# A decoder step on one core: the products with a pair of value pages are issued half a key step later

## The chip, the cores and the metric

The kernel runs on one core of a Trainium2 chip. The metric is device time in microseconds (us) of one execution, the median of several. The engines are TensorE (PE in the profile, with its weight loads as PEld), VectorE (DVE), ScalarE (ACT), GpSimd (POOL) and SyncE (SP). Each takes its instructions in a fixed order, and they wait for one another through semaphores. Sixteen DMA engines carry the transfers that the queues start.

## The reference, cut to what matters

One layer of a decoder is applied to two groups of rows with the same weights: a prompt of 1024 rows, and 8 samples of one row each. The samples attend to a paged cache of 8192 past tokens, 64 pages of 128 tokens for each sample, with 8 heads of 64 numbers:

```python
k_all = concatenate([k_pool[page_table], k]); v_all = concatenate([v_pool[page_table], v])
c = cumsum(concatenate([logf_pool[page_table], logf]))
s = einsum('bqhd,bkhd->bhqk', q, k_all) * HD**-0.5 + (c_q - c_k)
out = einsum('bhqk,bkhd->bqhd', softmax(s), v_all)
```

So for each sample all keys come first (scores), then a softmax over 8192 tokens, then all values (weighted sum). Keys and values of 8 samples are 256 blocks of 1 MB. The prompt goes through an input projection, causal attention, spatial gating, an output projection, cross-attention into 256 memory rows, and a gated MLP with a short convolution; the samples go through the same layers after their attention.

## The kernel before, in words

All is float32. The prompt's products are made of three matmuls each, of a rounded operand and its remainder (`gemm3`, lines 272 to 274); the weights come in blocks of 512 KB on SP's queue and are split by ACT (L235) and DVE (L236).

Two programs are woven into one. The prompt's, called the main program here, is a Python generator that goes through seven stages: p1 (input projection), att0 and attx, att1 (attention of the two halves of the rows), mid0 and ffn0 (projection, cross-attention and MLP of the first half), mid1 and ffn1 (the second). Each of its `yield`s hands over a label of how much TensorE time the step just issued is worth: 5.2 for a product with 24 matmuls of 512 columns, 3.9 for one of the down projection, 1 to 1.8 in attention. The samples' program is a second generator, called the decode, followed by the rest (the samples' other layers).

The loop at L1913 adds up the labels of the main program. When a stage's price (`PACE`, L76) has been reached, it takes one turn of the decode and subtracts the price times what that turn yields. Two limits matter here. A main step gives at most `int(t / price) + 1` turns, and while `held[0]` is set (around the norms) it gives none, so that labels pile up. The prices per whole step are 7.0 in p1, 12 in att0, 26 in attx, 11 in att1, 8.0 in mid0, 8.5 in ffn0, 6.8 in mid1, 2.5 in ffn1, and 2.9 for the rest.

The decode runs over `g` from 0 to 147. For each of the 8 samples there are 16 key steps. A key step (`kstep`, L1417) fetches 1 MB of keys by an indirect DMA on POOL's queue (L1420) and makes 4 x 8 scores for each partition on DVE: a multiply (L1436, or L1427 in attention) and a reduction (L1440, or L1428). In the attention stages it is cut into four parts with a yield of 0.2 before each; elsewhere it is one turn. Eighteen steps later come the values: after every second key step two blocks are fetched (`vstep`, L1479; its DMA is L1482), and the function that is to make their products is put on the list `pend`. In the next key step, behind that step's scores, both functions are called, the later block first. Each issues four column-tiled products (L1488) into one PSUM tile, `dv`. The turn then ends.

Keys and values share a ring of four 1 MB tiles (`KV`, tag `kv`). A fetch waits until a slot is free: a key's slot after its reduction on DVE, a value's after its products on PE. The fetches stand in POOL's queue in the order of the program.

Where an instruction lands within its engine's order is fixed at build time. `behind(engine)` (L1361) lets it stand no earlier than the main program's newest instruction on that engine; from there a planner with a simulated clock orders what is ready, by the order in which it was issued.

Of the kernel before, what the change touches and what calls it, by code (L numbers as in the profile page):

```python
# [78 lines left out]
def build(nc, tc, ctx, a, phases=None):  # L79
# [75 lines left out]
    def DV():  # L155
        return psum.tile([P, 512], F32, tag="dv", bufs=1, name=nm("dv"))
# [212 lines left out]
    def newest(e):  # L369

        return next(i for i in reversed(nc.cur_bb.bb.instructions) if i.engine == e)
# [994 lines left out]
    def decode():  # L1366
# [21 lines left out]
        def prep(b):  # L1388
            qb = D2()
            nc.sync.dma_start(qb, qs_d[b : b + 1, :].broadcast_to((P, 512)))  # L1390
            s = dpool.tile([P, 512], F32, tag="s", bufs=3, name=nm("s")).rearrange("p (k h) -> p k h", h=8)
            return qb, s

        def gates_scan(b):
            lg = D2()
            nc.gpsimd.indirect_dma_start(lg, None, a["cache_logf"], off(lidx[:, b : b + 1]))
            A = D2()
            Ah = A.rearrange("p (h k) -> p h k", k=64)
            nc.scalar.activation(Ah, lg.rearrange("p (k h) -> p h k", h=8), AF.Copy)
            nc.vector.tensor_tensor_scan(A, rmask, A, 0.0, op0=ALU.mult, op1=ALU.add)  # L1400
            return A

        def gates(b, A):
            tot = sm([P, 8], "tot", 2)
            nc.vector.tensor_tensor(
                tot, A.rearrange("p (h k) -> p h k", k=64)[:, :, 63], lfz[:, b * 8 : b * 8 + 8], op=ALU.add
            )
            ps = MS()
            with behind(ENG.PE):
                mmul(ps[:, :8], suf, tot, start=True, stop=True)  # L1410
            dt_ = dec("dec").rearrange("p (k h) -> p k h", h=8)
            nc.vector.tensor_tensor(
                dt_, ps[:, :8].unsqueeze(1).broadcast_to((P, 64, 8)), A.rearrange("p (h k) -> p k h", k=64), op=ALU.subtract
            )
            return dt_

        def kstep(b, ch, st):  # L1417
            qb, s = st
            kv = KV()
            nc.gpsimd.indirect_dma_start(kv, None, a["cache_k"], off(kidx[:, b, ch : ch + 1]))  # L1420
            kvv = kv.rearrange("p (k c) -> p k c", c=512)
            if phase[0][:3] == "att":

                for i in range(4):
                    yield 0.2
                    with behind(ENG.DVE):
                        nc.vector.tensor_tensor(kvv[:, i, :], kvv[:, i, :], qb, op=ALU.mult)  # L1427
                        nc.vector.tensor_reduce(  # L1428
                            s[:, ch * 4 + i, :], kvv[:, i, :].rearrange("p (h d) -> p h d", d=64), axis=AX.X, op=ALU.add
                        )  # L1430
                return 0.2
            sp = KS if phase[0][:3] == "mid" or held[0] else 1
            m = 4 // sp
            with behind(ENG.DVE):
                for i in range(0, 4, m):
                    nc.vector.tensor_tensor(  # L1436
                        kvv[:, i : i + m, :], kvv[:, i : i + m, :], qb.unsqueeze(1).broadcast_to((P, m, 512)), op=ALU.mult
                    )
                for i in range(0, 4, m):
                    nc.vector.tensor_reduce(  # L1440
                        s[:, ch * 4 + i : ch * 4 + i + m, :].rearrange("p k h -> p (k h)"),
                        kvv[:, i : i + m, :].rearrange("p k (h d) -> p (k h) d", d=64),
                        axis=AX.X,
                        op=ALU.add,
                    )
            return 1


        def soft_max(b, st, dt_):
            s = st[1]  # L1450
            with tc.high_priority():
                nc.vector.tensor_tensor(s, s, dt_, op=ALU.add)
                pm = sm([P, 8], "pm", 2)
                nc.vector.tensor_reduce(pm, s.rearrange("p k h -> p h k"), axis=AX.X, op=ALU.max)
            return pm

        def soft_all(b, pm):
            ps = MS()
            with behind(ENG.PE):
                nc.tensor.transpose(ps[:8, :P], pm, ident)  # L1460
            with tc.high_priority():
                m1 = sm([8, 1], "m1", 2)
                nc.vector.tensor_reduce(m1, ps[:8, :P], axis=AX.X, op=ALU.max)
                nc.vector.tensor_tensor(mT[:, b : b + 1], m1, snT[:, b : b + 1], op=ALU.max)
                dg = dgs[b % 2]
                nc.vector.tensor_scalar(dg[:8, :], ident[:8, :8], mT[:, b : b + 1], None, op0=ALU.mult)
            return dg

        def soft_exp(b, st, dg):
            s = st[1]  # L1470
            ps = MS()
            with behind(ENG.PE):
                mmul(ps[:, :8], ones, dg, start=True, stop=True)
            with tc.high_priority():
                nc.vector.tensor_tensor(s, s, ps[:, :8].unsqueeze(1).broadcast_to((P, 64, 8)), op=ALU.subtract)
                nc.scalar.activation(s, s, AF.Exp)
                nc.vector.tensor_reduce(lps[:, b, :], s.rearrange("p k h -> p h k"), axis=AX.X, op=ALU.add)

        def vstep(b, ch, st, dv):  # L1479
            s = st[1]  # L1480
            kv = KV()
            nc.gpsimd.indirect_dma_start(kv, None, a["cache_v"], off(kidx[:, b, ch : ch + 1]))  # L1482
            kvv = kv.rearrange("p (k c) -> p k c", c=512)

            def mm(after=None):
                with tc.issue_after(after) if after else behind(ENG.PE):
                    for j in range(4):
                        mmul(  # L1488
                            dv[32 * j : 32 * j + 32, :],
                            s[:, ch * 4 : ch * 4 + 4, :].rearrange("p k h -> p (k h)"),  # L1490
                            kvv[:, j, :],
                            start=(ch == 1),
                            stop=(ch == 14),
                            tile_position=(0, 32 * j),
                        )

            return mm

        def vmask(b, dv):
            vm = D2()  # L1500
            with tc.high_priority():
                nc.vector.tensor_tensor(
                    vm.rearrange("p (h d) -> p h d", d=64),
                    dv.rearrange("p (h d) -> p h d", d=64),
                    dm8.unsqueeze(2).broadcast_to((P, 8, 64)),
                    op=ALU.mult,
                )
            return vm

        def vend(b, vm):  # L1510
            nc.vector.tensor_reduce(vsum[:, b, :], vm.rearrange("p (h d) -> p d h", d=64), axis=AX.X, op=ALU.add)
# [8 lines left out]
        for g in range(8 * 16 + 16 + VLAG + 2):  # L1520
            b, ch = divmod(g, 16)
            if ch == VLAG + 1 and 2 <= b < 10:
                vend(b - 2, vm[b - 2])
            if ch == 0 and 1 <= b < 9:
                dg[b - 1] = soft_all(b - 1, pm[b - 1])
            if ch == 1 and 1 <= b < 9:
                soft_exp(b - 1, st[b - 1], dg[b - 1])
            left = 1
            if b < 8:
                left = yield from kstep(b, ch, st[b])  # L1530
                if ch == 11:
                    A[b] = gates_scan(b)
                if ch == 13:
                    dt_[b] = gates(b, A[b])
                if ch == 14 and b < 7:
                    st[b + 1] = prep(b + 1)
                if ch == 15:
                    pm[b] = soft_max(b, st[b], dt_[b])
            if pend:

                pend.pop()()
                pend.pop()(newest(ENG.PE))
                if vch == 15:
                    vm[vb] = vmask(vb, dv[vb])
            vb, vch = divmod(g - 16 - VLAG, 16)
            if 0 <= vb < 8 and vch % 2:
                if vch == 1:
                    dv[vb] = DV()
                pend += [vstep(vb, c, st[vb], dv[vb]) for c in (vch - 1, vch)]
            yield left  # L1550
# [354 lines left out]
    def sample():  # L1905
        yield from decode()
        phase[1] = "rest"
        yield from sample_rest()
# [116 lines left out]
```

## Time and profile before

| quantity | value |
|---|---|
| time, median of 3 runs | 1798.12 us (1797.17 to 1804.46) |
| the profiled execution's own time | 1804.14 us |
| its span, first to last instruction | 1802.1 us |
| PE busy | 1737.0 us (96%) |
| DVE busy | 1398.2 us (78%) |
| POOL busy | 506.6 us (28%) |
| moved by DMA | 521.06 MB, mean 289 GB/s |

The profile shows one execution. "Busy" is the time in which an engine had an instruction running; matmuls overlap, and their ends are modelled. In the groups of instructions a row names line, engine, operation and tiles, the count, the total and the mean time of one, and the idle time ahead of it with what ended it. The chain of waits follows back from the last instruction to what released it. In the timeline a row is a start, a duration, an engine, a line and an operation, and in brackets how long the engine had stood idle before it and what released it. The table of stretches gives for each stretch the busy time of PE, PEld, DVE, ACT and POOL with the instructions in brackets, then the granted TensorE clock, the DMA engines' busy share and the rate in GB/s.

### The profile page before, as it was taken

How to read it: one execution, taken by the hardware profiler on the slowest of the kernel's cores; microseconds unless marked ns; L12 is line 12 of the kernel's file. 1: busy time of each engine (PE TensorE's matmuls, PEld its weight loads, DVE VectorE, ACT ScalarE, POOL GpSimd, SP SyncE). 2: the span in 40 equal slices, each digit the busy share in tenths (PEclk: the TensorE clock that was granted, in tenths of full speed). 3: DMA queues.
4: the chain of work that ended last, by engine and by line, in shares of the span. 5: the costliest groups of instructions: out<-in, count | busy, mean ns of one | idle time of the engine just before them, and what ended most of it. 6: DMA issues, size and time to landing. Idle time of an engine off the chain costs nothing.

```text
span 1802.1 us, 25097 instructions
## 1 busy us (share of the span) xinstructions
PE 1737.0 (96%) x9637; PEld 1287.2 (71%) x9637; DVE 1398.2 (78%) x1729; ACT 736.4 (41%) x1378; POOL 506.6 (28%) x461
## 2 busy tenths in 40 slices
PE   8999999878999999999999999999989999999997
PEld 5887777555677667777777777776666778767875
DVE  4689658988788986999999999887875549855344
ACT  6332265465643635333333244336353323332332
POOL 1252333433123332332322223343422112002110
PEclk9999999999999999999999999999999999999999
DMA  8886888786697985778788778988879687568982
GB/s 296 301 298 226 300 317 329 265 273 212 223 407 277 355 331 217 290 291 341 296 305 309 290 302 321 377 304 325 308 276 338 224 297 249 185 260 299 357 312 82
DMA packets 157074, 521.06 MB, mean 289 GB/s; under 512 B 20874, under 2 KB 40842, under 8 KB 124186
## 3 DMA queue, kind: packets, MB, share of 16 engines
q0 software_dynamic: 57168, 341.14, 49.8%
q1 hardware_dynamic: 92874, 165.73, 26.7%
q10 hardware_dynamic: 6912, 12.59, 1.9%
q8 instruction: 76, 1.25, 0.3%
q14 instruction: 44, 0.36, 0.1%
HBM read 495.47 MB, written 23.93 MB: 288 GB/s over the span
## 4 chain that ended last, share of the span: by engine, by line
PE 47%; DMA 11%; issue 8%; DVE 6%; POOL 2%; ACT 1%; POOLq 0%; DVEq 0%
DMA kv<-cache_v,io 7%; PE ba L272 6%; PE ba L274 6%; PE ba L273 6%; PE dv L1488 3%; PE bb L272 3%; PE bb L274 3%; PE bb L273 3%; DMA kv<-cache_k,io 2%; DVE s L1440 2%; DVE kv L1436 1%; PE dv L331 1%; PE dv L1764 1%; POOL kv L1482 1%; POOL kv L1420 1%
## 5 line engine op out<-in xcount | busy, mean ns | idle before, releaser
L235 ACT ACTIVATE wh<-wr 128x1024 fp32r<-128x1024 f32 (+2 forms) x220 | 228.9, 1044 | 421.5 <-PE ba L273 138.8
L236 DVE TENSOR_TENSOR wl<-wr,wh 128x1024 fp32r<-128x1024 f32 (+2 forms) x220 | 262.9, 1199 | 172.6 <-PE ba L274 57.7
L1420 POOL DMA_INDIRECT kv<-cache_k,io x128 | 199.2, 1556 | 570.9 <-DVE s L1440 325.3
L1436 DVE TENSOR_TENSOR kv<-kv,d 128x1024 f32<-128x1024 f32 (+1 forms) x156 | 258.1, 1681 | 24.7 <-DMA kv<-cache_k,io 24.7
L1440 DVE TENSOR_REDUCE s<-kv 128x16 f32<-128x1024 f32 (+1 forms) x156 | 258.1, 1672 | 0.0
L1482 POOL DMA_INDIRECT kv<-cache_v,io x128 | 168.5, 1317 | 254.9 <-PE dv L1488 177.5
L272 PE MATMUL ba<-u,wh 128*128 128x512 f32 x528 | 209.3, 397 | 0.0
L273 PE MATMUL ba<-u,wh 128*128 128x512 f32 x528 | 208.8, 396 | 0.5 <-DVE u L239 0.5
L274 PE MATMUL ba<-u,wl 128*128 128x512 f32 x528 | 208.8, 396 | 0.0
L272 PE MATMUL ba<-wh,u 128*128 128x512 f32 (+1 forms) x495 | 186.4, 379 | 2.6 <-ACT u L235 2.6
L273 PE MATMUL ba<-wl,u 128*128 128x512 f32 (+1 forms) x495 | 185.1, 375 | 1.2 <-DVE wl L236 1.2
L274 PE MATMUL ba<-wh,u 128*128 128x512 f32 (+1 forms) x495 | 183.2, 375 | 0.0
L1488 PE MATMUL dv<-kv,s 128*32 128x512 f32 x1024 | 127.7, 606 | 3.6 <-DMA kv<-cache_v,io 3.5
L272 PEld LDWEIGHTS ba<-u,wh 128*128 128x128 f32 x528 | 99.5, 188 | 27.2 <-issue 5.6
L274 PEld LDWEIGHTS ba<-u,wl 128*128 128x128 f32 x528 | 99.3, 188 | 26.5 <-issue 4.0
L273 PEld LDWEIGHTS ba<-u,wh 128*128 128x128 f32 x528 | 99.3, 188 | 25.8 <-issue 3.1
L272 PEld LDWEIGHTS ba<-wh,u 128*128 128x128 f32 x495 | 93.0, 188 | 27.0 <-issue 6.5
L272 PE MATMUL bb<-u,wh 128*128 128x512 f32 x272 | 108.7, 400 | 0.0
L274 PE MATMUL bb<-u,wl 128*128 128x512 f32 x272 | 107.8, 397 | 0.0
L273 PE MATMUL bb<-u,wh 128*128 128x512 f32 x272 | 107.6, 396 | 0.0
L273 PEld LDWEIGHTS ba<-wl,u 128*128 128x128 f32 x495 | 93.0, 188 | 20.0 <-DVE wl L236 1.9
L274 PEld LDWEIGHTS ba<-wh,u 128*128 128x128 f32 x495 | 92.9, 188 | 19.5 <-issue 1.6
(445 smaller groups left out, 3313.8 us busy)
## 6 DMA issues: line engine op xcount, KB each, us to landing
wr<-w_up SPq DMA_DIRECT2D x88, 512.0 KB
kv<-w_up POOLq DMA_DIRECT2D x22, 1024.0 KB, 7.6
wr<-w_down SPq DMA_DIRECT2D x40, 512.0 KB
kv<-w_down POOLq DMA_DIRECT2D x11, 1024.0 KB, 8.3
wr<-w_in SPq DMA_DIRECT2D x16, 512.0 KB
wr<-w_o SPq DMA_DIRECT2D x16, 512.0 KB
wr<-w_cq SPq DMA_DIRECT2D x16, 512.0 KB
wr<-w_co SPq DMA_DIRECT2D x16, 512.0 KB
```

Source lines behind the costliest of these rows:

```text
L235: nc.scalar.activation(h, src, AF.Copy)
L236: nc.vector.tensor_tensor(l, src, h.bitcast(F32), op=ALU.subtract)
L272: mmul(out, sh, mh, start=(i == 0), stop=False)
L273: mmul(out, sh, ml, start=False, stop=False)
L274: mmul(out, sl, mh, start=False, stop=(i == n - 1))
L331: mmul(ps[32 * j : 32 * j + 32, :w], xT[:, k, :] if nk == 8 else xT[:, k * 8 : k * 8 + 32], raw[:, q, j * w : (j + 1) * w], start=(k == 0) ...
L1420: nc.gpsimd.indirect_dma_start(kv, None, a["cache_k"], off(kidx[:, b, ch : ch + 1]))
L1436: nc.vector.tensor_tensor(kvv[:, i : i + m, :], kvv[:, i : i + m, :], qb.unsqueeze(1).broadcast_to((P, m, 512)), op=ALU.mult)
L1440: nc.vector.tensor_reduce(s[:, ch * 4 + i : ch * 4 + i + m, :].rearrange("p k h -> p (k h)"), kvv[:, i : i + m, :].rearrange("p k (h d) -> ...
L1482: nc.gpsimd.indirect_dma_start(kv, None, a["cache_v"], off(kidx[:, b, ch : ch + 1]))
L1488: mmul(dv[32 * j : 32 * j + 32, :], s[:, ch * 4 : ch * 4 + 4, :].rearrange("p k h -> p (k h)"), kvv[:, j, :], start=(ch == 1), stop=(ch == ...
L1764: mmul(ps[32 * j : 32 * j + 32, :P], xsT[:, k, :], rvs[j // 2][:, k, j % 2, :], start=(k == 0), stop=(k == 7), tile_position=(0, 32 * j),)
```

## The change

The turn in which a pair's products are issued is cut in two. The scores' part of the key step ends with a yield of half of what was left of the step; the products are issued in the turn after that, which ends with a yield of the other half.

```diff
@@ -1538,6 +1538,8 @@
                     pm[b] = soft_max(b, st[b], dt_[b])
             if pend:
 
+                left /= 2
+                yield left
                 pend.pop()()
                 pend.pop()(newest(ENG.PE))
                 if vch == 15:
```

Outside the attention stages `left` is 1 there, so a step of 1 becomes 0.5 and 0.5; in attention it is 0.2, and becomes 0.1 and 0.1. No instruction is added or taken away. The 64 pairs of value blocks make 64 such turns. The masked copy of the finished sum (`vmask`, L1499) moves with the last products of each sample; the fetch of the next pair stays where it is in the program, behind the next key's fetch.

## The prediction

> **What bounds the kernel now.** First the page: busy times, the slices, and the groups of the decode.
>
> ```profile
> span 1802.1 us, 25097 instructions
> PE 1737.0 (96%) x9637; PEld 1287.2 (71%) x9637; DVE 1398.2 (78%) x1729; ACT 736.4 (41%) x1378; POOL 506.6 (28%) x461
> ...
> PE   8999999878999999999999999999989999999997
> DVE  4689658988788986999999999887875549855344
> ...
> L1440 DVE TENSOR_REDUCE s<-kv 128x16 f32<-128x1024 f32 (+1 forms) x156 | 258.1, 1672 | 0.0
> L1488 PE MATMUL dv<-kv,s 128*32 128x512 f32 x1024 | 127.7, 606 | 3.6 <-DMA kv<-cache_v,io 3.5
> ```
>
> PE is the bound: 96% busy, 65.1 us idle in all (1802.1 - 1737.0). The 1024 product matmuls that the change moves are 127.7 us of it, 2.0 us for each of 64 pairs. DVE has a 9 in most slices between 16 and 26, so there it is nearly a second bound.
>
> Then the table of stretches (columns PE, PEld, DVE, ACT, POOL, clock, DMA share, GB/s), to see where the idle time lies.
>
> ```profile
> 270.00:485.00 215.00, 188.30 (x1234) 133.18 (x1234) 184.09 (x325) 126.10 (x282) 74.34 (x102) 0.98 0.75 254
> 485.00:690.00 205.00, 202.61 (x1049) 147.06 (x1047) 177.41 (x219) 93.67 (x197) 69.68 (x47) 1.00 0.87 333
> 690.00:780.00 90.00, 87.57 (x417) 67.38 (x416) 80.65 (x91) 44.91 (x82) 26.93 (x20) 0.96 0.69 259
> 780.00:1080.00 300.00, 299.12 (x1414) 221.57 (x1413) 280.76 (x254) 99.74 (x150) 85.86 (x64) 1.00 0.82 310
> 1080.00:1330.00 250.00, 241.93 (x1193) 173.44 (x1191) 216.65 (x243) 103.79 (x213) 92.95 (x62) 0.99 0.88 326
> 1330.00:1415.00 85.00, 80.22 (x434) 54.77 (x431) 46.92 (x76) 34.04 (x62) 21.77 (x23) 0.96 0.84 309
> 1415.00:1802.00 387.00, 376.11 (x2540) 285.76 (x2538) 224.10 (x334) 122.58 (x221) 54.71 (x82) 0.99 0.68 248
> ```
>
> Attention (the first row) has 26.7 us of PE idle; the first half's projection and cross-attention 2.4; the way into its MLP 2.4; that MLP 0.9; the second half's stretch 8.1; its norm 4.8; the rest 10.9. While the decode runs in gemm stages PE has next to nothing to give back.
>
> Then the waits: PE's, POOL's, and DVE's for keys in the two cross-attention stretches (485 to 690, 1080 to 1330).
>
> ```profile
> PE ba L807 <- ACT wr L817: 6.8, 6, 1.9
> PE dv L1488 <- DMA kv<-cache_v,io: 3.5, 2, 3.0
> PE ba L273 <- DVE wl L236: 1.2, 3, 0.7
> ```
>
> ```profile
> POOL kv L1482 <- PE dv L1488: 177.5, 36, 17.2
> POOL kv L1420 <- PE dv L1488: 126.0, 18, 14.9
> ```
>
> ```profile
> DVE kv L1436 <- DMA kv<-cache_k,io: 3.2, 3, 1.9
> ```
>
> ```profile
> DVE kv L1436 <- DMA kv<-cache_k,io: 10.9, 5, 3.8
> ```
>
> PE waits for values only twice, 3.5 us together, and for split weights 1.2 us. It is POOL that waits for products (303.5 us), because a value's slot comes free with them; the fetches behind stand in its queue.
>
> **The change, part by part.** The sum is made against the profiled execution, 1804.14 us; the median, 1798.12, is 6.0 lower, and the prediction is brought down by that.
>
> *The work.* The same 1024 matmuls, 256 fetches and masks are issued: 0 us. On PE a pair goes from behind one main step to behind a later one. In ffn0 that looks like this now:
>
> ```profile
> 953.87 1.92 PE L1488 MATMUL dv<-kv,s 128*32 128x512 f32 x16
> 955.24 2.48 POOL L1420 DMA_INDIRECT kv<-cache_k,io  x1 [7.74 <-PE dv L1488]
> 958.03 0.94 POOL L1482 DMA_INDIRECT kv<-cache_v,io  x1 [0.30 <-issue]
> 959.27 2.10 POOL L1482 DMA_INDIRECT kv<-cache_v,io  x1 [0.30 <-issue]
> 965.19 0.94 POOL L1420 DMA_INDIRECT kv<-cache_k,io  x1 [3.83 <-DVE s L1440]
> ```
>
> A pair's period is 955.24 to 973.89 there by the next key fetch behind products, 18.7 us:
>
> ```profile
> 973.89 0.94 POOL L1420 DMA_INDIRECT kv<-cache_k,io  x1 [7.76 <-PE dv L1488]
> ```
>
> *Value fetches.* They wait for the products of the pair before. If both products move by one main step (label 5.2), so does the fetch between them, and the time that a value has to land stays a period less the products: 0 us. Below: the 3.5 us of waits could go. Above: where the planner moves the fetch but not the next products, up to 5.2 us each at the two places that wait already, +10.4. I take 0.
>
> *Key fetches behind them.* POOL is in order, and every second key stands behind a value pair. In ffn0 that key (965.19) had waited 3.83 us for DVE; values 5.2 us later would end POOL's second issue at 959.27 + 2.10 + 5.2 = 966.6, and the key goes at 966.9, 1.7 us late. In cross-attention there is less:
>
> ```profile
> 604.49 1.92 PE L1488 MATMUL dv<-kv,s 128*32 128x512 f32 x16
> 605.38 2.35 DVE L1436 TENSOR_TENSOR kv<-kv,d 128x1024 f32<-128x1024 f32 x2
> 605.86 2.71 POOL L1482 DMA_INDIRECT kv<-cache_v,io  x1 [2.63 <-PE dv L1488]
> 608.88 0.94 POOL L1482 DMA_INDIRECT kv<-cache_v,io  x1 [0.30 <-issue]
> 608.88 1.21 DVE L1440 TENSOR_REDUCE s<-kv 128x16 f32<-128x1024 f32 x1
> 612.62 2.81 POOL L1420 DMA_INDIRECT kv<-cache_k,io  x1 [2.79 <-DVE s L1440]
> 622.97 2.36 DVE L1436 TENSOR_TENSOR kv<-kv,d 128x1024 f32<-128x1024 f32 x2 [1.89 <-DMA kv<-cache_k,io]
> ```
>
> Values end 5.2 later at 615.0, the key goes at 615.3 in place of 612.6: 2.7 us late, and its multiply at 622.97 waits for it already. In the two stretches 3 + 5 keys come late today (rows above). How many pairs there are is in the table of stretches for the products' line alone (16 matmuls to a pair; the first row is attention):
>
> ```profile
> 270.00:485.00 215.00, 15.39 (x128) 3.33 (x128) 0.98 0.75 254
> 485.00:690.00 205.00, 21.46 (x175) 4.72 (x176) 1.00 0.87 333
> 1080.00:1330.00 250.00, 29.58 (x224) 6.13 (x224) 0.99 0.88 326
> ```
>
> That is 11 + 14 = 25 pairs with 50 keys, of which 8 have no cover, one in six. 25 / 6 = 4 pairs x 2.7 = 11 us more of DVE waiting. DVE is idle for 27.6 + 33.4 us in those stretches, and today's 14.1 us of key waits go with 0.7 us of PE waiting for weights at the most at one time, so most of it is absorbed: a quarter taken, +3 us. Below 0 (nothing reaches PE), above all 25 pairs with half of it reaching PE, 25 x 2.7 / 2 = +34.
>
> The two value issues at 605.86 and 608.88 differ by 1.8 us: the longer ran beside DVE's multiply, the shorter beside a reduction. [...]
>
> *The turns.* Outside attention a pair's two steps now need 3 turns, not 2, and with 5.2 per main step and a price above it `int(5.2 / 8.5) + 1` allows one. So two steps need 15.6 of main labels. Due are 2 x 8.5 = 17.0 in ffn0 and 16.0 in mid0, where it suffices, 14.0 in p1 and 13.6 in mid1, where the decode falls behind, and in all of them debt from a held stretch is paid more slowly. Following the loop's counters along the main program's 478 steps (1445.4 of labels), the decode's last turn comes at label 1142.8 and not 1127.2; the rest, which then has more debt and two turns per step, ends at 1421.0 and not 1424.9. So the end is not moved, and a lag of 15.6 would also be covered there:
>
> ```profile
> 1777.43 0.31 SPq L1818 DMA_DIRECT2D o_ys<-vsum  x1
> 1789.02 8.62 SPq L1354 DMA_DIRECT2D o_y<-u  x5
> ```
>
> The samples' last store is issued at 1777.4 and the prompt's from 1789.0 to 1797.6, 20.2 us later at the end. I take 0; above, a lag of twice 15.6 would put 31.2 - 20.2 = +11 behind the end.
>
> *Attention.* A step's last 0.2 becomes 0.1 and 0.1, so the products move by about one main step (1.8) of a price of 11 to 26. PE is idle 26.7 us there for ACT's exponentials (L807 above), and eight pairs (128 matmuls, 15.4 us) stand among them. Best case all eight fill a gap that they don't fill now, -15; worst case all leave one, +15. Nothing in the rows says which: 0.
>
> Sum: 1804.14 + 0 + 0 + 3 + 0 + 0 = 1807, less 6.0 makes 1801. About 0.5% (9 us) is what a measurement of this kernel can tell from no change, so the forecast is no change: 1789 to 1807.
>
> **The rivals.** *Keys starve DVE, slower.* Place: POOL's queue in the two cross-attention stretches. If values move later in most pairs, the uncovered keys are not 4 but 16; 16 x 2.7 = 43 us of DVE waiting, and half reaches PE through the split weights that stand behind in DVE's order: +21, 1798 + 21 = 1819. It decides once the added DVE waiting passes the 61 us idle only in sum, but in place whatever a few weights ahead cover. For it: DVE's 1.89 us wait above, and 94% busy in ffn0 (280.76 of 300). Against: in ffn0 PE stands 0.9 us idle with that load.
>
> [...]
>
> *Smoother catching up, faster.* After a hold, debt was paid at a step per 5.2 of main work; a step is 2 x 2.28 us or more of DVE (258.1 us in 156 reductions, as much in multiplies, 4.0 us per step), so DVE had little left for the main program. At 7.8 per step it has. It can win the idle time next to holds, 2.4 + 2.4 + 8.1 + 4.8 = 17.7 us, and some of the 0.04 of clock; two thirds is -12: 1786. Against: PE's named waits there are on ACT and values, hardly on DVE.
>
> *The rest comes too late, slower.* +11: 1809. Against: the counters.
>
> *The change does little.* `behind` only sets the earliest place; where values land later than that the planner has put the products at the landing already. That time is inside the forecast.
>
> **How the numbers follow.** No change, with the last rival, 0.50; keys starving 0.25; smoother 0.20; rest late 0.05. Faster 0.20, same 0.50, slower 0.30. The range reaches from the smoother case, 1786, to the starving one, 1819; it leaves out what lies beyond these, about 0.2.
>
> **What would show it.** The rows of POOL waiting for products and of DVE waiting for keys in the two stretches: 14.1 us now, about 25 by the sum, over 50 by the first rival. PE's idle time, 65.1, should be 62 to 75. PE's 127.7 us of products should stay. The samples' last store should stand 10 us or more before the prompt's. The prediction is wrong if PE idles over 80 us, or under 55, or if the planner makes another order in attention that is worth more than the 15 us allowed there.

## The result, and the profile after

| | median, us | runs | ratio to before (95%) |
|---|---|---|---|
| before | 1798.12 (1794.46 to 1804.46) | 5 | |
| after | 1832.84 (1831.40 to 1835.62) | 5 | 1.0174 (1.0154 to 1.0194) |

The change costs 34.7 us, 1.7%. The forecast was no change, and the time lies outside the range that went with it. The profiled execution took 1831.40 us, 27.3 more than that of before (1804.14), which was 6.0 above its median, while this one is 1.4 below.

First the page after: totals, the slices of PE and DVE, and the groups of the decode that the prediction read.

```profile
span 1829.6 us, 25082 instructions
PE 1749.4 (96%) x9637; PEld 1293.7 (71%) x9637; DVE 1397.3 (76%) x1727; ACT 739.0 (40%) x1380; POOL 510.0 (28%) x461
...
PE   8999999789999999999999999999999999999998
DVE  4689667888778887898989899988875549854345
...
L1440 DVE TENSOR_REDUCE s<-kv 128x16 f32<-128x1024 f32 (+1 forms) x159 | 260.7, 1656 | 0.0
L1488 PE MATMUL dv<-kv,s 128*32 128x512 f32 x1024 | 129.6, 604 | 0.3 <-DMA kv<-cache_v,io 0.3
```

The span is 27.5 us longer, and it splits into two halves. PE stands idle for 80.2 us (1829.6 - 1749.4), 15.1 more than before. And it is busy for 12.4 us more with the same 9637 matmuls, which then ran more slowly (the mean granted clock is 0.984, and was 0.991). The table of stretches shows where (columns PE, PEld, DVE, ACT, POOL, granted clock, DMA share, GB/s).

```profile
270.00:485.00 215.00, 185.91 (x1147) 131.69 (x1146) 175.54 (x312) 120.47 (x272) 75.17 (x99) 0.92 0.74 251
485.00:690.00 205.00, 191.21 (x996) 137.04 (x995) 166.78 (x211) 89.23 (x188) 57.57 (x42) 0.98 0.79 301
...
780.00:1080.00 300.00, 300.00 (x1410) 223.88 (x1409) 279.03 (x252) 100.67 (x152) 95.59 (x64) 1.00 0.81 303
```

In attention 1147 matmuls are done where 1234 were. PE's idle time hardly grows there, from 26.7 to 29.1 us (215.00 - 185.91), but the granted clock is 0.92 in place of 0.98. The next stretch does 996 in place of 1049; there it is the idle time that grows, from 2.4 to 13.8 us (205.00 - 191.21). The MLP of the first half (780 to 1080) shows no idle time and full clock. The lag along the program is read from the first and the last start of the same lines (the numbers ahead of and behind "to"; before, then after).

```profile
L1064 PE MATMUL ba<-wh,u x96: 387/395/796, 492.5 to 1302.0; 128*128 128x512 f32 x96
L1200 PE MATMUL ba<-cp,u x40: 272/273/421, 609.4 to 1271.7; 128*128 128x128 f32 x40
L1354 SPq DMA_DIRECT2D o_y<-u x10: 332/332/450, 1135.7 to 1797.3; - x10
```

```profile
L1064 PE MATMUL ba<-wh,u x96: 387/395/798, 508.5 to 1329.7; 128*128 128x512 f32 x96
L1200 PE MATMUL ba<-cp,u x40: 272/273/417, 632.6 to 1300.3; 128*128 128x128 f32 x40
L1354 SPq DMA_DIRECT2D o_y<-u x10: 332/356/357, 1162.8 to 1824.8; - x10
```

By the first half's projection (L1064) the program is 16.0 us late, in its cross-attention (L1200) 23.2, at the first of its stores (L1354) 27.1 and at the last 27.5. From 632.6 us on, less than 5 us are added, against a profile that was itself 6.0 us above its median. Most is lost in attention and in the 130 us that follow it.

Last the waits: PE's, and DVE's for keys in the two cross-attention stretches.

```profile
PE bb L836 <- ACT t L814: 6.6, 5, 2.6
PE ms L872 <- ACT t L861: 2.6, 1, 2.6
PE ba L274 <- DVE wl L236: 2.6, 1, 2.6
```

```profile
DVE kv L1436 <- DMA kv<-cache_k,io: 13.4, 3, 7.4
```

```profile
DVE kv L1436 <- DMA kv<-cache_k,io: 13.2, 5, 5.5
```

PE does not wait for values any more (0.3 us). What has come or grown is a handful of waits of 2 to 3 us each for an operand from ACT or DVE, spread over attention and what follows it (the first of these rows stood at 2.9 us before, the others did not have a wait of this length).

### The profile page after: what moved, and what is told of

It is laid out like the page before. It is cut to its first block, busy times and chain, and to the rows that moved or that the text cites. A ratio compares the mean times of both kernels' runs of the same rounds, so it can differ in the third digit from the quotient of the medians.

```text
span 1829.6 us, 25082 instructions
## 1 busy us (share of the span) xinstructions
PE 1749.4 (96%) x9637; PEld 1293.7 (71%) x9637; DVE 1397.3 (76%) x1727; ACT 739.0 (40%) x1380; POOL 510.0 (28%) x461
## 4 chain that ended last, share of the span: by engine, by line
PE 51%; DVE 8%; issue 8%; DMA 5%; POOL 2%; ACT 2%; POOLq 0%; DVEq 0%; SPq 0%; ACTq 0%
PE ba L274 7%; PE ba L272 7%; PE ba L273 6%; PE dv L1488 4%; PE bb L272 3%; DMA kv<-cache_k,io 3%; PE bb L274 3%; PE bb L273 3%; PE ba L1064 1%; PE ba L1065 1%; PE ba L1066 1%; DVE s L1440 1%; PE dv L331 1%; PE dv L1766 1%; DVE kv L1436 1%
## 5 line engine op out<-in xcount | busy, mean ns | idle before, releaser
L1420 POOL DMA_INDIRECT kv<-cache_k,io x128 | 192.3, 1503 | 506.6 <-DVE s L1440 332.2
L1482 POOL DMA_INDIRECT kv<-cache_v,io x128 | 178.3, 1393 | 321.8 <-PE dv L1488 228.3
L1488 PE MATMUL dv<-kv,s 128*32 128x512 f32 x1024 | 129.6, 604 | 0.3 <-DMA kv<-cache_v,io 0.3
L272 PEld LDWEIGHTS ba<-u,wh 128*128 128x128 f32 x528 | 99.7, 189 | 29.1 <-issue 4.6
```

Source lines behind the costliest of these rows:

```text
L272: mmul(out, sh, mh, start=(i == 0), stop=False)
L1488: mmul(dv[32 * j : 32 * j + 32, :], s[:, ch * 4 : ch * 4 + 4, :].rearrange("p k h -> p (k h)"), kvv[:, j, :], start=(ch == 1), stop=(ch == ...
```

## The experiments

Each ratio is to the kernel before in the same runs on the same chip.

**Which stage.** The cut was made in the attention stages only, outside of them only, and in the second attention stage only.

```diff
             if pend:
-                left /= 2
-                yield left
+                if phase[0][:3] == "att":      # gemm_only: != "att";  att1_only: phase[0] == "att1"
+                    left /= 2
+                    yield left
```

> The turn is cut in two in the attention stages alone; everywhere else the products stay at the key step's beginning. Two losses (attention's own, about 12 us, and one in the first half's projection, about 14 us, made by a hold that falls between scores and products): 1798 + 12 = 1810. One loss (all of it comes out of attention and is only seen later): 1832. Turns (what costs is that a pair takes three turns and not two): in attention a pair takes 11 and not 10, so little, 1798 to 1803.

> The turn is cut in two everywhere but in the attention stages. Two losses: attention is as before, the hold still falls between step 46's scores and its products or makes the pairs behind it late, 1798 + 10 to 15 = 1808 to 1813. One loss out of attention: 1798. Turns: nearly the whole loss, 1825 to 1832.

> The turn is cut in two in the second attention stage alone. Edge: nothing of the loss, 1798 to 1803, since step 31 is past. Attention as such (later products leave PE waiting for exponentials and its clock halved): half of the loss or more, 1810 to 1825.

Measured: attention only 1832.13 us, 1.0170 (1.0129 to 1.0211); outside only 1807.67, 1.0029 (1.0012 to 1.0045); second attention stage only 1801.45, 0.9988 (0.9974 to 1.0001). Attention carries 30.2 of the 34.7 us, and as its second stage alone costs nothing, the first one (att0, with attx between the two) does. The 56 pairs outside attention, on which most of the prediction was spent, cost 5.8.

**What in that stage.** The products stay behind their step's scores and only the second turn is kept (two_turns); the kernel before gets one or two empty turns and nothing else (lost_turn_1, lost_turn_2); the cut stays, but its second half may be taken while the main program is held (hold_exempt) or does not count against a main step's limit on turns (cap_free).

```diff
# two_turns
                 pend.pop()()
                 pend.pop()(newest(ENG.PE))
                 if vch == 15:
                     vm[vb] = vmask(vb, dv[vb])
+                left /= 2
+                yield left
# lost_turn_1 (kernel before; lost_turn_2: g in (28, 30))
+            if g == 30:
+                yield 0.0
# hold_exempt, split_[0] is true in the second half
-        while bgs and not held[0] and most and ...
+        while bgs and (not held[0] or split_[0]) and most and ...
# cap_free
-            most -= 1
+            most -= not split_[0]
```

> The turn is cut in two, but the products are issued ahead of the cut, where they were before: the count of turns and the pace of the changed kernel, the place of the products of the kernel before. Turns: 1825 to 1835. Place (attention) and hold: neither is there, 1795 to 1803.

> The kernel before with one empty turn, at the end of key step 30. Key step 31 still ends ahead of the jump (main step 85 and not 84), but key step 32 starts behind it (95 and not 85). Edge, if step 31's end and its softmax are what counts: 1798 to 1806. If the start of step 32 is what counts: 1822 to 1832.

> The kernel before, with two empty turns added, one each at the end of key steps 28 and 30; nothing else is touched, and the products stay at the key step's beginning. By the loop's counters key step 31 ends at main step 92, as in the changed kernel, and not at 84. Edge: 1822 to 1832 without any of the change. Place: 1798 to 1803.

> The changed kernel, but a second half of a cut turn may be taken while the loop is on hold, so no hold can fall between a step's scores and its products. Two losses: the hold's part goes, 1832 - 14 = 1818. One loss out of attention, or turns: 1832.

> The changed kernel, but the second half of a cut turn does not count against the one turn that a main step may give. The products keep their later place; key step 31 gets back its place ahead of the jump of the price from 12 to 26. Edge (the eleventh turn makes the decode lose two main steps in the first attention stage, and key step 31 with its softmax falls behind the jump): 1800 to 1808. Place or chance reshuffling of the order: stays at 1825 to 1832.

| run | median, us | ratio (95%) |
|---|---|---|
| two_turns | 1827.31 | 1.0142 (1.0102 to 1.0183) |
| lost_turn_1 | 1821.85 | 1.0091 (1.0055 to 1.0126) |
| lost_turn_2 | 1828.46 | 1.0117 (1.0084 to 1.0151) |
| hold_exempt | 1829.47 | 1.0125 (1.0076 to 1.0173) |
| cap_free | 1825.43 | 1.0119 (1.0095 to 1.0143) |

The hold is not needed for the loss. Nor is the place of the products within their key step by itself: with that place as before and one turn lost (lost_turn_1) the time is 18 us up. Nor is it the lost turns by themselves: cap_free loses none, moves only products, and is 21 us up. Whatever displaces the decode in the first attention stage costs about the same, 18 to 28 us.

The time need not be lost where the displacement is made. In lost_turn_1 the first L1064 starts at 493.6 us (492.5 before), the first L1200 at 619.1 (609.4), and the last store is issued at 1818.1 (1797.3): it is 1.1, then 9.7, then 20.8 us late, nearly all of it behind attention.

By the loop's counters, att0 gives the decode one turn per main step at most, so a lost turn is a main step lost. In the changed kernel key step 31 takes its last turn at main step 92 and not 84, behind the point where the price jumps from 12 to 26, and the sample's softmax falls among attx's exponentials. The whole change, the cut in attention only, two_turns, hold_exempt and lost_turn_2 all show the same three waits there; before, lost_turn_1 and cap_free, whose step 31 ends at 84 or 85, do not. Lost_turn_2 as an example, PE's waits from 320 to 370 us:

```profile
PE ms L1460 <- DVE pm L1454: 3.0, 1, 3.0
PE bb L836 <- ACT t L814: 2.8, 3, 2.0
PE ba L807 <- DVE wr L659: 1.9, 1, 1.9
```

That is some 7 us; behind the longest of the waits for t (2.0 us) seven matmuls of 512 columns also take 0.63 us each in place of 0.40. It does not explain the two runs without these waits.

**How small a displacement is enough.** Only one pair's products, in attx, moved (attx_only); the three pairs of att0 moved one main step later and nothing else (att0_free, as cap_free but in att0 only); the first of those three alone (p26_free); and the three moved one main step earlier (early_1).

```diff
# attx_only
+                if phase[0] == "attx":
                     left /= 2
                     yield left
# att0_free: if phase[0] == "att0":    p26_free: if g == 26:
+                    left /= 2
+                    split_[0] = True
+                    yield left
+                    split_[0] = False
# early_1 (kernel before): in att0, ahead of the step's last quarter
+                    if n == 3 and pend and phase[0] == "att0":
+                        pend.pop()()
+                        pend.pop()(newest(ENG.PE))
```

> The cut is made only in stage attx, where it moves one pair's products (those of key step 32) from the 108th to the 110th step of the main program; no fetch and no score moves. Theory lag (the loss comes because work of the decode stands later than before where the price jumps from 12 to 26): this pair stands right behind the jump, so it alone should cost 8 to 18 us, 1810 to 1822. Theory one place (the loss sits in att0 itself): 1800 to 1806. Theory brittle order (any displacement in att0 or attx lets the planner make another order, of which most are worse): anywhere from 1800 to 1825, but the places where TensorE goes idle need not be those of the full change.

> The cut is made only in stage att0, and its second half takes no turn of the main step: the products of key steps 26, 28 and 30 stand one step of the main program later (59, 70, 80 in place of 58, 69, 79), and nothing else moves. Theory lag at the jump: nothing stands later at the jump, so 1800 to 1806. Theory one place (att0): 1815 to 1828, most of the loss of the change. Theory brittle order: 1810 to 1828.

> As the run before, but for key step 26 alone: eight matmuls stand one step of the main program later, 59 in place of 58, and nothing else in the program moves. Theory lag and theory one place (a lateness that adds up over the stage): 1800 to 1808. Theory brittle order: as likely 1815 to 1825 as 1802, since one displaced instruction is enough to make another order.

> The kernel before, with the products of key steps 26, 28 and 30 one step of the main program earlier (ahead of the last quarter of their key step), nothing else moved. Theory lag, in either place: earlier is not later, so 1798 to 1806, no loss. Theory brittle order: a loss of the same kind as for later products, 1810 to 1825, with more stretches of half clock in attention and more idle time of TensorE, or by luck 1800.

| run | median, us | ratio (95%) |
|---|---|---|
| attx_only | 1800.14 | 0.9996 (0.9976 to 1.0016) |
| att0_free | 1809.29 | 1.0051 (1.0033 to 1.0069) |
| p26_free | 1811.44 | 1.0056 (1.0036 to 1.0077) |
| early_1 | 1805.85 | 1.0016 (0.9998 to 1.0034) |

One pair's products, eight in the program, which the profile shows as sixteen matmuls, and some 2 us of TensorE, one main step later: 10 us. That rules out a lag behind the price jump as the only cause, since nothing stands later there. The theory that any other order is a worse one is not borne out either: for earlier products the interval does not exclude nothing, and the pair in attx is free. There is something particular about that place. The timeline of p26_free (the lines behind 1007 stand one further down; POOL issues, SP issues, ACT, PE):

```profile
279.86 1.49 POOL L1483 DMA_INDIRECT kv<-cache_v,io  x1 [0.17 <-PE dv L1489]
...
286.66 1.00 POOL L1421 DMA_INDIRECT kv<-cache_k,io  x1 [0.66 <-DVE s L1429]
287.97 0.97 POOL L1421 DMA_INDIRECT kv<-cache_k,io  x1 [0.30 <-DVE mx L813]
290.64 4.53 SPq L249 DMA_DIRECT2D wr<-w_cv  x4
300.88 1.06 ACT L235 ACTIVATE wh<-wr 128x1024 fp32r<-128x1024 f32 x1 [4.96 <-DMA wr<-w_cv]
301.84 0.67 ACT L814 ACTIVATE t<-ba,mx 128x512 f32<-128x512 f32 x1
302.65 1.12 PE L836 MATMUL bb<-cp,t 128*128 128x128 f32 x4 [5.93 <-ACT t L814]
303.70 3.64 PE L1489 MATMUL dv<-kv,s 128*32 128x512 f32 x16
```

The same place before:

```profile
276.79 1.07 POOL L1482 DMA_INDIRECT kv<-cache_v,io  x1 [6.63 <-PE dv L1488]
...
289.34 1.44 POOL L1420 DMA_INDIRECT kv<-cache_k,io  x1 [2.57 <-DVE mx L813]
289.95 5.56 SPq L249 DMA_DIRECT2D wr<-w_cv  x4
291.08 0.96 POOL L1420 DMA_INDIRECT kv<-cache_k,io  x1 [0.30 <-DVE wl L236]
293.54 1.06 ACT L235 ACTIVATE wh<-wr 128x1024 fp32r<-128x1024 f32 x1
294.50 0.67 ACT L814 ACTIVATE t<-ba,mx 128x512 f32<-128x512 f32 x1
296.99 1.92 PE L1488 MATMUL dv<-kv,s 128*32 128x512 f32 x16
```

The values' fetches wait for the displaced products, so they start 3.1 us later; the keys' start 2.7 us earlier. The two value and two key blocks of 1 MB each, whose issues were spread over 14.3 us, are issued within 8.1. The first of the four weight blocks that SP asks for from 290.64 us on is split by ACT at 300.88, 10.2 us later; before, the block asked for at 289.95 was being split after 3.6 us. In ACT's order the softmax's exponential (L814), for which PE waits 5.93 us, stands next behind the split: in both kernels it starts 0.96 us after the split does. The stretches of p26_free from 290 to 310 us (the granted clock is 0.92, then 0.57):

```profile
290.00:300.00 10.00, 6.72 (x40) 5.21 (x38) 5.97 (x10) 4.44 (x6) 0.00 (x0) 0.92 0.98 358
300.00:310.00 10.00, 7.34 (x29) 3.59 (x30) 4.34 (x8) 2.67 (x6) 1.86 (x2) 0.57 0.70 237
```

The DMA engines are 98% busy from 290 to 300 us, and in the next ten, of which the first 2.65 are the rest of PE's wait, the mean granted clock is 0.57. The sixteen products behind the wait take 3.64 us and took 1.92. They end 8.4 us later than before (307.3 and 298.9), while SP's first issue stood 0.7 us later: 7.7 of the 10 us arise in this place.

In the DMA view of 289 to 301 us POOL's queue q0 and SP's q1 stand so:

```profile
q0 software_dynamic: 409, 2.41, 54.1%
q1 hardware_dynamic: 713, 1.39, 32.0%
```

These sums alone do not tell the two kernels apart: in the same 12 us of before q0 moved 2.20 MB and q1 1.32. What differs is what was moved first. In the 3 us from SP's issue on, the DMA view of p26_free (290.64 to 293.64) has the gathers' queue and no packet of q1; the one of before (289.95 to 292.95) has nearly the whole block:

```profile
q0 software_dynamic: 114, 0.85, 82.5%
```

```profile
q1 hardware_dynamic: 248, 0.50, 54.1%
```

So in p26_free SP's block did not share the DMA engines with the four fetches at first; for 3 us it got nothing.

**The test of that reading.** To p26_free something is added that changes only the moment of the key fetches: eight small powers on POOL, whose first waits for the same scores as the fetch of key step 28, stand ahead of that fetch. The order of instructions on ACT and PE stays that of p26_free, and so does DVE's but for one clearing of the small tile that the powers use. The same eight were put into cap_free (free_delay), where the cut is made in every stage.

```diff
+            if (b, ch) == (1, 12):
+                for i in range(8):
+                    nc.gpsimd.tensor_tensor(scr[:, i : i + 1], scr[:, i : i + 1], s[:, 43, i : i + 1], op=ALU.pow)
             nc.gpsimd.indirect_dma_start(kv, None, a["cache_k"], off(kidx[:, b, ch : ch + 1]))
```

> As the run that displaced the products of key step 26 alone (1811 us), with eight one-column powers on the otherwise idle POOL (128x1, about 1 us each) ahead of the key fetch of step 28. The orders of ACT, TensorE and, but for one clearing of the small tile, DVE are the same as in that run, so nothing but the moment of the key fetches differs. Theory bunching (the fetches of two value blocks and two key blocks, issued within 8 us just ahead of it, keep the 512 KB block of w_cv issued at 290.6 us away until 300.9, ACT stands for it with the softmax's exponential behind it, and TensorE goes dry): the key fetches now come behind the weight block, ACT's wait of 4.96 us goes to at most 1.5, TensorE's of 5.93 to at most 2, and the time to 1800 to 1806. Theory order (the exponential stands behind one weight split more, whatever is fetched): ACT's order is the same, so the wait stays at 4 to 6 us and the time at 1809 to 1813; with the keys late in addition it could be longer.

> The whole change with its second halves free of the limit on turns (1825 us), and the eight powers on POOL ahead of the key fetch of step 28. The orders of ACT, TensorE and, but for one clearing, DVE are those of that run. Theory bunching: the waits that disappeared from the small run disappear here too (ACT for the block of w_cv 5.2 us, TensorE behind it 6.15 us, 6.8 us at half clock), 8 to 11 us less: 1813 to 1818, and what is left of the loss sits behind 490 us. If the collision mattered only because the rest of that run was undisturbed: 1822 to 1828.

Measured: p26_delay 1803.62 us, 1.0016 (0.9999 to 1.0032), where p26_free had 1.0056 (1.0036 to 1.0077). Added work on POOL, ahead of a fetch that DVE waits for, made the kernel 8 us faster. In its trace:

```profile
287.25 5.87 POOL L1423 TENSOR_TENSOR scr<-scr,s 128x1 f32<-128x1 f32 x8 [0.53 <-DVE s L1432]
291.34 4.54 SPq L249 DMA_DIRECT2D wr<-w_cv  x4
293.29 1.75 POOL L1424 DMA_INDIRECT kv<-cache_k,io  x1 [0.18 <-issue]
296.51 1.06 ACT L235 ACTIVATE wh<-wr 128x1024 fp32r<-128x1024 f32 x1
297.45 0.69 ACT L814 ACTIVATE t<-ba,mx 128x512 f32<-128x512 f32 x1
298.29 0.66 PE L836 MATMUL bb<-cp,t 128*128 128x128 f32 x4 [0.86 <-ACT t L814]
```

The weight block now goes ahead of the keys (in its first 3 us q1 moves 0.49 MB), ACT splits it without waiting, and PE's 5.93 us have become 0.86. As ACT's and PE's orders are the same, it was the moment of the fetches and not the order that cost the 8 us; the 2.0 us that are left cannot be told from nothing. In cap_free the same eight powers took the median from 1825.43 to 1818.02, 7.4 us; the ratio, 1.0102 (1.0069 to 1.0134) after 1.0119 (1.0095 to 1.0143), does not separate them, while in the two traces the span went from 1821.4 to 1812.9 and PE's wait there from 6.15 to 2.1 us. So the collision seems to count there too, but at about a third of what that version loses.

**Do the parts add up?** The whole change except in att0 and attx.

```diff
+                if phase[0] not in ("att0", "attx"):
                     left /= 2
                     yield left
```

> The whole change but for stages att0 and attx. If the two stages carry the loss and the other parts add up (5.7 us outside attention, 2.5 us less from att1): 1800 to 1808. If the parts do not add up, because att1 and the stages behind it only behave when the order ahead of them is that of before: 1812 or more.

Measured 1809.94 us, 1.0058 (1.0039 to 1.0076). The two parts that it joins came to 5.8 and -2.5 us; together they cost 8.3. They do not quite add up, but without the first attention stage the change costs 8 us and with it 35.

**What the changed kernel itself loses by.** It has p26_free's displacement and more, but its fetches fall differently and ACT's longest wait for w_cv there is 1.19 us. So the collision that was tested is not what the changed kernel loses by. PE's waits in the rows below are 2.6 to 3.0 us each. Rows of its timeline:

```profile
336.63 0.55 PE L836 MATMUL bb<-cp,t 128*128 128x128 f32 x3 [2.62 <-ACT t L814]
...
364.08 0.38 PE L1460 MATMUL ms<-cp,pm 128*8 128x128 f32 x1 [3.01 <-DVE pm L1454]
...
503.88 1.06 ACT L235 ACTIVATE wh<-wr 128x1024 fp32r<-128x1024 f32 x1 [2.48 <-DMA wr<-w_o]
505.84 0.44 PE L872 MATMUL ms<-cp,t 128*128 128x128 f32 x2 [2.64 <-ACT t L861]
...
587.95 2.36 DVE L1436 TENSOR_TENSOR kv<-kv,d 128x1024 f32<-128x1024 f32 x2 [7.39 <-DMA kv<-cache_k,io]
596.06 2.34 DVE L236 TENSOR_TENSOR wl<-wr,wh 128x1024 fp32r<-128x1024 f32 x2
597.32 0.80 PE L274 MATMUL ba<-u,wl 128*128 128x512 f32 x1 [2.58 <-DVE wl L236]
```

At 505 us ACT stands for a block of w_o with the operand of a last product of attention behind it. At 588 DVE stands 7.39 us for a key, does what stands behind it in its order, and reaches the remainder of a weight late: PE waits 2.58 us for it and then runs at a granted clock of 0.50 until 600.26 us (the next matmuls of 512 columns take 0.63 us and not 0.40). These places were read, not tested. That each of them goes back to a bunching of fetches is a guess, and one reading speaks against it as the common cause: from 270 to 700 us ACT stands 13.4 us for weight blocks in the kernel before and 25.4 in the changed one, but only 8.8 with the cut in attention alone and 6.0 in lost_turn_1, which lose 30 and 18 us.

## Why the prediction was wrong

- *Attention: 0, between -15 and +15.* This is the step that failed. The cut in attention alone costs 30.2 us. It bounded the eight pairs by their own 15.4 us of work, which at worst would leave PE's gaps. What a product's place does to others was put at nothing: one pair with 2 us of work costs 10 when it is moved alone, because the value fetch that waits for it came 3.1 us later, the key fetches 2.7 earlier, and ACT then stood 4.96 us for the weight block behind them. In the changed kernel itself that collision is absent; there attention's loss shows as a clock of 0.92 in place of 0.98, and the next stretch's as 11.4 us more of idle time. The prediction followed the queues behind a moved product in the gemm stages and not here. It also had the move too small, "about one main step": by the loop's counters the eight pairs stand 1, 1, 2, 5, 2, 3, 3 and 3 main steps later.
- *The turns: 0.* Worked out for the stages outside attention, where it holds or nearly does (5.8 us, with the key fetches). In att0, where one turn per main step is the limit already, it was left out. By the counters step 31 ends eight main steps later, and three waits of 7 us together go with that.
- *The clock.* It entered only as a part of the 0.04 that the rival of smoother catching up might win. In the changed kernel slow matmuls are 12.4 us of the 27.5, about as much as the idle time.
- *Key fetches behind them: +3.* 14.1 us of DVE waits became 26.6 (13.4 + 13.2), with about 25 expected, but that is luck in good part. With the cut outside attention alone, which is what the term was about, the same two rows give 18.4 (10.8 + 7.6), 4.3 more where 11 were expected; and with the products issued ahead of the cut (two_turns) they give 22.0. What reaches PE was near, as the cut outside attention costs 5.8 where 3 were taken.
- *Keys starve DVE, 1819.* Its mechanism is in the trace at 588 to 597 us, once, not in the number that it was priced for.
- *Value fetches: 0.* Right for PE: its waits for values went from 3.5 to 0.3 us.
- *The work, the rest and the end.* Right: the products take 129.6 us (127.7 before), and the samples' last store is issued at 1805.39 us, 19.4 ahead of the prompt's last at 1824.8.
- *What would make it wrong* named both that came: PE idle over 80 us (80.2), and another order in attention worth more than 15 us.

What is settled: most of the loss comes with what is displaced in the first attention stage, a displacement of 16 matmuls there costs 10 us, and 8 of these go away when the key fetches are kept off the weight block. Why the whole change costs 35 us stays open: how its loss splits over the smaller waits and the slow clock, and how much of it is bunching of fetches, the softmax of a sample among the prompt's, or something else that comes with another order.

## What to carry to other kernels

A step that frees a buffer also sets the moment of the fetch that waits for it (here the values' fetches started 3.1 us later): when it is moved, follow that fetch, see what else is on its way then, and look for an engine in whose order a transfer's reader stands ahead of what the matmuls need (here ACT stood 4.96 us for a weight block, and PE 5.93 for the exponential behind it). In a stage where TensorE hangs on short chains through other engines, price a moved step by those chains and by the slow clock that can follow a gap (sixteen products took 3.64 us in place of 1.92 behind one of 5.93), and not by its own work. And when a small change costs much, cut it down until one displacement is left: the cause of 10 us could be read in eight rows, that of 35 could not.

## What had not been expected of the hardware

- A 512 KB block was split 3.6 us after its issue in one kernel and 10.2 us in another; what differed was whether the 1 MB fetches had been issued just ahead of it or around it and behind it.
- In the 3 us behind its issue the block had 248 packets moved in the first of these kernels and none in the second, where the 1 MB fetches ahead of it had 114.
- The slow clock can add much to the price of a gap: behind 5.93 us of idle time sixteen products took 3.64 us in place of 1.92, where the granted clock of the ten us around them was 0.57. In the changed kernel the extra busy time, 12.4 us, nearly equals the extra idle time, 15.1. But it does not follow every gap: behind 2.64 us of waiting, at 506 us, sixteen products took 1.92, while behind 2.58, at 597 us, matmuls took 0.63 in place of 0.40. From 596.84 to 600.26, for 3.42 us, the granted clock was 0.50; in as long a stretch ahead of that (593.43 to 596.84) PE was busy for 1.31 us, at a clock of 1.00. Around the gap that had no drop two such stretches have 1.92 us (501.27 to 504.68) and 2.26 (504.68 to 508.10) of busy time, both at a clock of 1.00.
- Eight one-column powers on POOL took 5.87 us, 0.73 each, and made the kernel 8 us faster.
